# Byte offsets of TensorE's operands in SBUF: equal steps for the weight slots, h shifted by 16 bytes from FFN to FFN, each buffer of g by 32 bytes

## The chip, the cores and the metric

The kernel runs on one core of one Trainium2 chip. The metric is the device time of the whole program in microseconds, the median of several runs. One execution was also recorded by the hardware profiler.

## The reference, cut to what matters

The program is a decoder trunk of two layers on 512 tokens of 1024 channels. Each layer is an FFN, a token mixer and another FFN; the first mixer is a causal pooling, the second an attention with a forget gate. A norm with shift and scale stands before each of the six sublayers, numbered 0 to 5, so that the FFNs are 0, 2, 3 and 5, the pooling is 1 and the attention is 4:

```
h = rms_norm(x) * gain * (1 + scale) + shift
x = x + 0.5 * (1 + gate) * ((silu(h @ w_g) * (h @ w_u)) @ w_out)        # FFN, width 2816
```

All of it is in float32.

## The kernel before

**Precision.** A matmul takes float32r operands, of fewer bits than float32. Every operand is therefore split into a high part (rounded) and a low part (the rest), and `mm3` (lines 162 to 165) makes three matmuls of each product: high weight with high data (L163), high weight with low data (L164), low weight with high data (L165). The standing operand, 128 x 128, is loaded ahead of each matmul; the streaming operand has 512 or 256 columns.

**Layout.** Channels lie on the 128 partitions, tokens along the free dimension. h, the normed input, is a pair of tiles `hhi` and `hlo` of 8 blocks of 512 tokens; `norm` (lines 210 to 220) writes them in two halves of 256 tokens. g, the gated hidden values, is a pair of tiles of 512 tokens for each of the 22 blocks of the FFN's width, in nine rotating buffers each for the high and the low part.

**An FFN** (`ffn`, from line 258, and `closing`) goes through the width in three chunks of 8, 8 and 6 blocks. In `up` each block is 48 matmuls: gate and up projection, 8 blocks of channels, three products; the text calls these 48 a column block. The first two or three blocks of FFNs 2, 3 and 5 are done in two halves of 256 tokens, all others in 512 columns. After a chunk, the down product streams g: for each of 8 output blocks 24 matmuls. The last chunk's down product, `closing`, has 18 matmuls for each output block, in two halves of 256 columns (FFN 5: one of 512).

**Weights** come from DRAM to a `raw` tile, and ScalarE and VectorE split them into a slot, a pair of tiles `wh` and `wl` of 8 KB a partition each (`slot`, lines 67 to 71). FFNs 0, 2 and 3 rotate over three slots, two in the pool `wts` and one in the pool `more`; FFN 5 and the attention rotate over the two of `wts`. The first four blocks of FFN 0 use these three and a fourth pair, `w4`. In the attention the projections to q, k and v have h standing and the weights streaming, 256 columns wide; the forget gate has its weights `fh` and `fl` standing and h streaming.

**Where tiles lie.** Pools are stacked in the order in which they are opened, from the left (low addresses) or the right (high addresses), each tile on a multiple of 32 bytes. From the right: `top` with h, then `right` with `cond` (4096 bytes), then `more`. From the left: `pers`, `tmp`, `wts`, then the pools of each stage, g's among them. The start addresses that follow, in bytes of a partition, with the remainder modulo 512:

| tiles | address | modulo 512 |
|---|---|---|
| hhi, hlo | 196576, 212960 | 480 |
| wh, wl of the two slots in `wts` | 43808, 52000, 60192, 68384 | 288 |
| wh, wl of the slot in `more` | 176096, 184288 | 480 |
| g, first buffer (FFNs 0 and 2; 3 and 5) | 92960; 125728 | 288 |
| first weights of the attention, `w` | 92960 and on | 288 |
| fh, fl | 145248, 149344 | 352 |
| w4 | 154432, 162624 | 320 |

Block strides inside these tiles (512 bytes for the FFNs' weights, 1024 for those of the projections, 2048 for h and g's buffers) keep the remainder.

**Order.** SyncE's queue, which issues all DMAs, is in the order of the program's text in the FFNs; the other engines' order is a scheduler's, by a modelled timeline, except for the beginning, where ScalarE and VectorE are in the order of the text too.

Of the kernel before, what the change touches and what calls it, by code (L numbers as in the profile page):

```python
# [7 lines left out]
F32 = mybir.dt.float32  # L8
F32R = mybir.dt.float32r
# [6 lines left out]
P = 128  # L16
D = 1024
KT = D // P
S = 512
# [3 lines left out]
JC = 8  # L23
# [10 lines left out]
LAG = 3  # L34
SPAN = 16
EARLY = 4
WHOLE = ((0, S),)
HALVES = ((0, S // 2), (S // 2, S // 2))

# [2 lines left out]
def trunk(  # L42
# [6 lines left out]
    pe, act, dve, gp = nc.tensor, nc.scalar, nc.vector, nc.gpsimd  # L49

    top = ctx.enter_context(tc.tile_pool(name="top", bufs=1, side="right"))
    hhi = top.tile([P, KT, S], F32R, name="hhi")
    hlo = top.tile([P, KT, S], F32R, name="hlo")
    adas = ExitStack()
    right = adas.enter_context(tc.tile_pool(name="right", bufs=1, side="right"))
    pers = ctx.enter_context(tc.tile_pool(name="pers", bufs=1))
    tmp = ctx.enter_context(tc.tile_pool(name="tmp", bufs=2))
    wts = ctx.enter_context(tc.tile_pool(name="wts", bufs=2))
    ps = ctx.enter_context(tc.tile_pool(name="ps", bufs=5, space=PSUM))
    pss = ctx.enter_context(tc.tile_pool(name="pss", bufs=3, space=PSUM))  # L60
# [3 lines left out]
    def bank(tag="mm"):  # L64
        return banks[tag].tile([P, S], F32, tag=tag, name=tag)
# [89 lines left out]
    def weights(src, shape, pieces=4):  # L155
        raw = wts.tile(shape, F32, tag="raw", name="raw")
        nc.sync.dma_start(raw, src)
        parts = slot(shape)
        split(parts, raw, pieces)
        return parts  # L160

    def mm3(o, lh, ll, rh, rl, start, stop):
        pe.matmul(o, lh, rh, start=start, stop=False)  # L163
        pe.matmul(o, lh, rl, start=False, stop=False)  # L164
        pe.matmul(o, ll, rh, start=False, stop=stop)  # L165
# [42 lines left out]
        return r  # L208

    def norm(i, acc, t0, tn, summed=False):  # L210
        sl = slice(t0, t0 + tn)
        r = rsig(acc, t0, tn, summed)
        for kt in range(KT):
            a, s = (mods[i][c][:, kt:kt + 1] for c in "as")
            t1 = tmp.tile([P, tn], F32, tag="t1", name="t1")
            dve.scalar_tensor_tensor(out=t1, in0=x[:, kt, sl], scalar=a, in1=r[:, :tn],
                                     op0=ALU.mult, op1=ALU.mult)
            act.activation(hhi[:, kt, sl], t1, AF.Identity, bias=s)
            dve.scalar_tensor_tensor(out=hlo[:, kt, sl], in0=t1, scalar=s,
                                     in1=hhi[:, kt, sl].bitcast(F32), op0=ALU.add, op1=ALU.subtract)  # L220
# [11 lines left out]
    def new_acc():  # L232
        return tmp.tile([P, S], F32, tag="acc", name="acc", bufs=1)
# [24 lines left out]
    def ffn(i, feed, jobs, then, begin=None, ahead_by=2, started=None):  # L258
        jobs = list(jobs)
        loaded = []  # L260

        def job(pool, behind):

            if loaded:
                work, raw = loaded.pop()
                with tc.issue_after(behind):
                    work(raw)
                if ahead_by == 1:
                    return
            if jobs:  # L270
                load, work = jobs.pop(0)
                loaded.append((work, load(pool)))

        acc = new_acc() if then else None
        with (
            tc.tile_pool(name=f"ffn{i}", bufs=2, reuse_waits="tile") as fp,
            tc.manual_schedule(engines={mybir.EngineType.SP}),
            ExitStack() as early,
        ):
            ap = early.enter_context(tc.tile_pool(name=f"ada{i}", bufs=ahead_by, reuse_waits="tile"))  # L280

            def g_tile():
                return (fp.tile([P, S], F32R, tag="gh", name="gh", bufs=JC + 1),
                        fp.tile([P, S], F32R, tag="gl", name="gl", bufs=JC + 1))

            def gated(gu, g, t0, tn):
                sl = slice(t0, t0 + tn)
                sil = fp.tile([P, S], F32, tag="sil", name="sil")
                act.activation(sil[:, :tn], gu[0][:, :tn], AF.Silu)  # L289
                dve.tensor_tensor(out=sil[:, :tn], in0=sil[:, :tn], in1=gu[1][:, :tn], op=ALU.mult)  # L290
                act.activation(g[0][:, sl], sil[:, :tn], AF.Copy)  # L291
                return dve.tensor_tensor(out=g[1][:, sl], in0=sil[:, :tn], in1=g[0][:, sl].bitcast(F32),
                                         op=ALU.subtract)

            def up(wt, g, t0, tn):
                wh, wl = wt
                sl = slice(t0, t0 + tn)
                gu = []
                for k in range(2):
                    o = bank()  # L300
                    for kt in range(KT):
                        mm3(o[:, :tn], wh[:, k, kt], wl[:, k, kt], hhi[:, kt, sl], hlo[:, kt, sl],
                            kt == 0, kt == KT - 1)
                    gu.append(o)
                return gated(gu, g, t0, tn)

            for ci, (j0, nj) in enumerate(CHUNKS):
                g = []
                ready = 0
                if ci == 0:  # L310
                    ready = started or feed.depth
                    g = [g_tile() for _ in range(ready)]
                    if begin is not None:
                        begin(g, gated)
                        feed.fetch(feed.depth)
                        nc.sync.dma_start(x, x_in)
                        job(ap, None)
                    else:
                        head, feed.made = feed.made, []
                        for t0, tn in HALVES:  # L320
                            for j in range(ready):
                                up(head[j], g[j], t0, tn)
                                if t0:
                                    feed.fetch()
                for j in range(j0 + ready, j0 + nj):
                    wt = feed.take()
                    g.append(g_tile())
                    done = up(wt, g[-1], 0, S)
                    if j >= 3:
                        job(ap, done.ins)  # L330
                if ci < 2:
                    for dt in range(KT):
                        wh, wl = feed.take()
                        y = bank()
                        for f in range(nj):
                            mm3(y, wh[:, f], wl[:, f], g[f][0], g[f][1], f == 0, f == nj - 1)
                        done = dve.scalar_tensor_tensor(  # L337
                            out=x[:, dt, :], in0=y, scalar=mods[i]["g"][:, dt:dt + 1],
                            in1=x[:, dt, :], op0=ALU.mult, op1=ALU.add)
                        job(ap, done.ins)  # L340
                else:
                    while jobs or loaded:
                        job(ap, done.ins)
                    early.close()
                    feed.fetch(len(feed.units))
                    closing(feed.made, 6, g, i, acc, then)

    def closing(wt, n, g, i, acc, then):

        for t0, tn in HALVES if then else WHOLE:  # L350
            sl = slice(t0, t0 + tn)
            for dt in range(KT):
                y = bank()
                for f in range(n):
                    (wh, wl), at = wt[(dt * n + f) // 16], (dt * n + f) % 16
                    mm3(y[:, :tn], wh[:, at], wl[:, at], g[f][0][:, sl], g[f][1][:, sl], f == 0,
                        f == n - 1)
                update(y[:, :tn], i, dt, t0, tn, acc)
            if then:
                then(acc, t0, tn)  # L360
# [88 lines left out]
    def fox(i, early_pool, first, second_half, then):  # L449
        acc2 = new_acc()  # L450
        with tc.tile_pool(name="fox", bufs=1, reuse_waits="tile") as fp:
# [205 lines left out]
            def early(ots):  # L657
# [3 lines left out]
                def step(dt):  # L661
                    y = bank("s")
                    for k in range(EARLY):
                        u, at = divmod(dt * EARLY + k, 16)
                        if at == 0:
                            held["w"] = weights(fox_o[u], [P, 16, P])
                        wh, wl = held["w"]
                        mm3(y, wh[:, at], wl[:, at], ots[k][0], ots[k][1], k == 0, k == EARLY - 1)
                    dve.scalar_tensor_tensor(
# [13 lines left out]
            for grp in range(NG):  # L683
                nxt, steps = projections(grp + 1) if grp + 1 < NG else (None, [])
                if grp == NG - 1:
                    steps = early(ots)
                    ots = ots[EARLY:]
                ots += attend(made, grp, steps)
                made = nxt
            closing([weights(fox_o[u], [P, 16, P]) for u in range(EARLY // 2, KT // 2)], KT - EARLY,  # L690
                    ots, i, acc2, then)
# [3 lines left out]
    with tc.tile_pool(name="more", bufs=1, side="right", reuse_waits="tile") as more:  # L695
# [78 lines left out]
        def begin(g, gated):  # L774
            for j in range(4):
                gated(gu[j], g[j], 0, S)
# [118 lines left out]
```

## Time and profile before

| | us |
|---|---|
| median of three runs (lowest, highest) | 1857.13 (1853.2, 1859.62) |
| profiled execution | 1856.85 |
| its span, first to last instruction | 1855.1 |
| TensorE busy with matmuls | 1822.1 (98%) |
| weight loads, beside the matmuls | 1543.5 (83%) |
| VectorE, ScalarE, GpSimd busy | 985.9, 622.5, 106.9 |

The mean granted clock of TensorE is 0.99 of full speed. The chain of work that ended last is 96% TensorE, 85% of it in the three lines of `mm3` with banks of the tag `mm`. [...]

### The profile page before, as it was taken

How to read it: one execution, taken by the hardware profiler on the slowest of the kernel's cores; microseconds unless marked ns; L12 is line 12 of the kernel's file. 1: busy time of each engine (PE TensorE's matmuls, PEld its weight loads, DVE VectorE, ACT ScalarE, POOL GpSimd, SP SyncE). 2: the span in 40 equal slices, each digit the busy share in tenths (PEclk: the TensorE clock that was granted, in tenths of full speed). 3: DMA queues.
4: the chain of work that ended last, by engine and by line, in shares of the span. 5: the costliest groups of instructions: out<-in, count | busy, mean ns of one | idle time of the engine just before them, and what ended most of it. 6: DMA issues, size and time to landing. Idle time of an engine off the chain costs nothing.

```text
span 1855.1 us, 23985 instructions
## 1 busy us (share of the span) xinstructions
PE 1822.1 (98%) x9564; PEld 1543.5 (83%) x9564; DVE 985.9 (53%) x1947; ACT 622.5 (34%) x1242; POOL 106.9 (6%) x118
## 2 busy tenths in 40 slices
PE   6999999989999999999999999999999999999999
PEld 5888888879888888998888889988997888888887
DVE  7467466386466473363554534666676653432433
ACT  6323223244213232242222333354444442222221
POOL 0000000040000000110000001321010200000000
PEclk9999999989999999999999999999999899999999
DMA  9457466211366452131543431022211121321321
GB/s 365 183 202 265 174 234 225 92 69 66 117 252 243 171 216 94 69 137 69 204 164 131 183 126 69 33 70 80 69 64 63 38 100 57 127 102 56 136 92 68
DMA packets 45712, 244.66 MB, mean 132 GB/s; under 512 B 5392, under 2 KB 9872, under 8 KB 21792
## 3 DMA queue, kind: packets, MB, share of 16 engines
q1 hardware_dynamic: 45600, 243.13, 35.8%
q8 instruction: 75, 1.23, 0.3%
q14 instruction: 37, 0.30, 0.0%
HBM read 240.98 MB, written 2.13 MB: 131 GB/s over the span
## 4 chain that ended last, share of the span: by engine, by line
PE 96%; DVE 2%; ACT 0%; DMA 0%; issue 0%; SPq 0%; POOL 0%; ACTq 0%; POOLq 0%
PE mm L163 29%; PE mm L164 28%; PE mm L165 28%; PE s L163 3%; PE s L164 3%; PE s L165 3%; PE mm L600 1%; PE mm L583 1%; PE mm L422 1%; DVE wl L152 1%; DMA rows<-x_rows 0%; DVE x L225 0%; PE s L543 0%; PE mm L181 0%; DVE win L396 0%; PE s L207 0%
## 5 line engine op out<-in xcount | busy, mean ns | idle before, releaser
L164 PE MATMUL mm<-hlo,wh 128*128 128x512 f32 (+1 forms) x1512 | 566.0, 376 | 2.5 <-DVE hlo L764 2.5
L165 PE MATMUL mm<-hhi,wl 128*128 128x512 f32 (+1 forms) x1512 | 564.5, 376 | 0.5 <-DVE wl L152 0.5
L163 PE MATMUL mm<-hhi,wh 128*128 128x512 f32 (+1 forms) x1512 | 560.1, 375 | 1.8 <-ACT hhi L755 1.4
L151 ACT ACTIVATE wh<-raw 128x256 fp32r<-128x256 f32 (+2 forms) x528 | 311.3, 654 | 572.4 <-PE mm L164 324.5
L152 DVE TENSOR_TENSOR wl<-raw,wh 128x256 fp32r<-128x256 f32 (+2 forms) x528 | 359.8, 733 | 50.5 <-ACT wh L151 46.4
L164 PEld LDWEIGHTS mm<-hlo,wh 128*128 128x128 f32 x1512 | 284.3, 188 | 58.7 <-DVE hlo L764 3.0
L165 PEld LDWEIGHTS mm<-hhi,wl 128*128 128x128 f32 x1512 | 284.5, 188 | 56.5 <-DVE wl L152 0.7
L163 PEld LDWEIGHTS mm<-hhi,wh 128*128 128x128 f32 x1512 | 282.5, 188 | 58.2 <-ACT hhi L755 1.8
L290 DVE TENSOR_TENSOR sil<-sil,mm 128x512 f32<-128x512 f32 (+1 forms) x95 | 61.0, 642 | 481.1 <-PE mm L165 473.3
L164 PE MATMUL mm<-gl,wh 128*128 128x512 f32 (+1 forms) x848 | 299.1, 353 | 0.0
L165 PE MATMUL mm<-gh,wl 128*128 128x512 f32 (+1 forms) x848 | 298.0, 353 | 0.0
L163 PE MATMUL mm<-gh,wh 128*128 128x512 f32 (+1 forms) x848 | 297.8, 354 | 0.0
L165 PEld LDWEIGHTS mm<-gh,wl 128*128 128x128 f32 x848 | 159.9, 189 | 22.4
L164 PEld LDWEIGHTS mm<-gl,wh 128*128 128x128 f32 x848 | 160.0, 189 | 22.2
L163 PEld LDWEIGHTS mm<-gh,wh 128*128 128x128 f32 x848 | 159.3, 189 | 22.7
L100 DVE CUSTOM_DVE_ANT_0 ada<-ada,cond 128x1024 f32<-128x1024 f32 x144 | 170.1, 1218 | 0.7 <-DMA ada<-ada_w 0.7
L289 ACT ACTIVATE sil<-mm 128x512 f32<-128x512 f32 (+1 forms) x94 | 52.7, 561 | 254.6 <-PE mm L165 253.3
L337 DVE SCALAR_TENSOR_TENSOR x<-mm,mg,x 128x512 f32<-128x512 f32 x64 | 47.9, 749 | 105.3 <-PE mm L165 104.8
L175 POOL TENSOR_TENSOR acc<-acc,sq 128x256 f32<-128x256 f32 x56 | 49.5, 884 | 870.9 <-ACT sq L174 535.3
L163 PE MATMUL s<-wh,hhi 128*128 128x256 f32 x288 | 84.0, 292 | 1.9 <-DVE qk L549 1.9
L291 ACT ACTIVATE gh<-sil 128x512 fp32r<-128x512 f32 (+1 forms) x96 | 56.1, 585 | 76.6 <-DVE sil L290 76.6
L165 PE MATMUL s<-wh,hlo 128*128 128x256 f32 x288 | 81.6, 283 | 0.0
(177 smaller groups left out, 1728.3 us busy)
## 6 DMA issues: line engine op xcount, KB each, us to landing
raw<-w_in SPq DMA_DIRECT2D x84, 1024.0 KB, 5.0
ada<-ada_w SPq DMA_DIRECT2D x72, 1024.0 KB, 4.9
raw<-w_out SPq DMA_DIRECT2D x64, 512.0 KB, 5.6
raw<-w_end SPq DMA_DIRECT2D x12, 1024.0 KB, 4.8
raw<-fox_qkv SPq DMA_DIRECT2D x12, 1024.0 KB, 4.8
raw<-w_in SPq DMA_DIRECT2D x16, 256.0 KB, 8.3
cb<-cum SPq DMA_DIRECT2D x16, 256.0 KB, 3.3
raw<-fox_o SPq DMA_DIRECT2D x4, 1024.0 KB, 4.9
```

The costliest lines, as they stand in the source:

```text
L100: dve.tensor_tensor_reduce(out=raw[:, r, :], in0=raw[:, r, :], in1=cond, scale=1.0, scalar=0.0, op0=ALU.mult, op1=ALU.add, accum_out=mods[ ...
L151: act.activation(hi[:, c:c + n], src[:, c:c + n], AF.Copy)
L152: dve.tensor_tensor(out=lo[:, c:c + n], in0=src[:, c:c + n], in1=hi[:, c:c + n].bitcast(F32), op=ALU.subtract)
L163: pe.matmul(o, lh, rh, start=start, stop=False)
L164: pe.matmul(o, lh, rl, start=False, stop=False)
L165: pe.matmul(o, ll, rh, start=False, stop=stop)
L175: gp.tensor_tensor(out=acc[:, sl], in0=acc[:, sl], in1=sq, op=ALU.add)
L289: act.activation(sil[:, :tn], gu[0][:, :tn], AF.Silu)
L290: dve.tensor_tensor(out=sil[:, :tn], in0=sil[:, :tn], in1=gu[1][:, :tn], op=ALU.mult)
L291: act.activation(g[0][:, sl], sil[:, :tn], AF.Copy)
L337: done = dve.scalar_tensor_tensor(out=x[:, dt, :], in0=y, scalar=mods[i]["g"][:, dt:dt + 1], in1=x[:, dt, :], op0=ALU.mult, op1=ALU.add)
L422: pe.matmul(y[:, :tn], self.w[:, 2 * dt + ct], made[dt // 2][:, ct], start=ct == 0, stop=ct == 1)
```

## The change

Three things are done, all to where tiles lie. An unused tile of 48 floats, `gap`, stands between `tmp` and `wts`. h becomes one tile, `h_room`, longer by 16 floats, from which `h_tiles` cuts the pair at a start that depends on the sublayer: float 16 (FFN 0 and the attention), 12 (FFN 2), 8 (FFN 3), 4 (FFN 5). The buffers of g are longer by 8 floats, and the 512 that are used begin at float 0, 2, 4 or 6 in FFNs 0, 2, 3 and 5.

```
--- before.py
+++ after.py
@@ -34,6 +34,10 @@
 LAG = 3
 SPAN = 16
 EARLY = 4
+H_ROOM = 16
+H_AT = {2: 12, 3: 8, 5: 4}
+G_ROOM = 8
+G_AT = {0: 0, 2: 2, 3: 4, 5: 6}
 WHOLE = ((0, S),)
 HALVES = ((0, S // 2), (S // 2, S // 2))
 
@@ -49,12 +53,21 @@
     pe, act, dve, gp = nc.tensor, nc.scalar, nc.vector, nc.gpsimd
 
     top = ctx.enter_context(tc.tile_pool(name="top", bufs=1, side="right"))
-    hhi = top.tile([P, KT, S], F32R, name="hhi")
-    hlo = top.tile([P, KT, S], F32R, name="hlo")
+    h_room = top.tile([P, 2 * KT * S + H_ROOM], F32R, name="h")
+
+    def h_tiles(i):
+
+        at = H_AT.get(i, H_ROOM)
+        both = h_room[:, at:at + 2 * KT * S].rearrange("p (c k t) -> p c k t", c=2, t=S)
+        return both[:, 0], both[:, 1]
+
+    hhi, hlo = h_tiles(0)
     adas = ExitStack()
     right = adas.enter_context(tc.tile_pool(name="right", bufs=1, side="right"))
     pers = ctx.enter_context(tc.tile_pool(name="pers", bufs=1))
     tmp = ctx.enter_context(tc.tile_pool(name="tmp", bufs=2))
+    gap = ctx.enter_context(tc.tile_pool(name="gap", bufs=1))
+    gap.tile([P, 48], F32, name="gap")
     wts = ctx.enter_context(tc.tile_pool(name="wts", bufs=2))
     ps = ctx.enter_context(tc.tile_pool(name="ps", bufs=5, space=PSUM))
     pss = ctx.enter_context(tc.tile_pool(name="pss", bufs=3, space=PSUM))
@@ -208,6 +221,9 @@
         return r
 
     def norm(i, acc, t0, tn, summed=False):
+        nonlocal hhi, hlo
+        if t0 == 0:
+            hhi, hlo = h_tiles(i)
         sl = slice(t0, t0 + tn)
         r = rsig(acc, t0, tn, summed)
         for kt in range(KT):
@@ -280,8 +296,8 @@
             ap = early.enter_context(tc.tile_pool(name=f"ada{i}", bufs=ahead_by, reuse_waits="tile"))
 
             def g_tile():
-                return (fp.tile([P, S], F32R, tag="gh", name="gh", bufs=JC + 1),
-                        fp.tile([P, S], F32R, tag="gl", name="gl", bufs=JC + 1))
+                return [fp.tile([P, S + G_ROOM], F32R, tag=t, name=t, bufs=JC + 1)[:, G_AT[i]:G_AT[i] + S]
+                        for t in ("gh", "gl")]
 
             def gated(gu, g, t0, tn):
                 sl = slice(t0, t0 + tn)
```

## Rows read from the trace of the kernel before

**Rows 1.** The page: the span, and TensorE's share of it.

```profile
span 1855.1 us, 23985 instructions
...
PE 1822.1 (98%) x9564; PEld 1543.5 (83%) x9564; DVE 985.9 (53%) x1947; ACT 622.5 (34%) x1242; POOL 106.9 (6%) x118
```

**Rows 2.** TensorE's waits: us, times, longest; the longest, and that for h.

```profile
PE s L738 <- DVE rows L745: 12.1, 1, 12.1
...
PE mm L163 <- ACT hhi L218: 0.2, 1, 0.2
```

**Rows 3.** Windows: busy (count), clock, DMA share, GB/s; around pooling, FFN 2, 5.

```profile
357.00:462.00 105.00, 97.56 (x686) 0.93 0.18 62
462.00:758.00 296.00, 296.00 (x1288) 1.00 0.48 181
1508.00:1852.00 344.00, 343.41 (x1487) 1.00 0.27 94
```

**Rows 4.** Groups of TensorE by form: busy us, mean ns; h and g.

```profile
L163 PE MATMUL mm<-hhi,wh 128*128 128x512 f32 x1256 | 491.7, 394 | 1.4 <-ACT hhi L755 1.4
...
L163 PE MATMUL mm<-gh,wh 128*128 128x512 f32 x560 | 217.8, 390 | 0.0
```

**Rows 5.** Timeline (start, duration), FFN 2: column blocks, 48 matmuls apart.

```profile
472.99 0.40 PE L163 MATMUL mm<-hhi,wh 128*128 128x512 f32 x1
...
484.19 0.40 PE L163 MATMUL mm<-hhi,wh 128*128 128x512 f32 x1
...
495.38 0.39 PE L163 MATMUL mm<-hhi,wh 128*128 128x512 f32 x1
...
506.29 0.40 PE L163 MATMUL mm<-hhi,wh 128*128 128x512 f32 x1
```

**Rows 6.** Timeline, FFN 5, h on both slots, 192 matmuls apart.

```profile
1518.71 0.39 PE L163 MATMUL mm<-hhi,wh 128*128 128x512 f32 x1
...
1563.51 0.39 PE L163 MATMUL mm<-hhi,wh 128*128 128x512 f32 x1
```

**Rows 7.** Timeline, FFN 2, g on `wts`, then on `more`, 24 apart.

```profile
533.93 0.39 PE L163 MATMUL mm<-gh,wh 128*128 128x512 f32 x1
...
539.37 0.39 PE L163 MATMUL mm<-gh,wh 128*128 128x512 f32 x1
...
544.87 0.39 PE L163 MATMUL mm<-gh,wh 128*128 128x512 f32 x1
```

**Rows 8.** Timeline, FFN 2, h, 256: 24 on `wts`, 18 `more`, 24 `wts`.

```profile
439.57 0.28 PE L163 MATMUL mm<-hhi,wh 128*128 128x256 f32 x1
...
442.29 0.28 PE L163 MATMUL mm<-hhi,wh 128*128 128x256 f32 x1
...
445.01 0.28 PE L163 MATMUL mm<-hhi,wh 128*128 128x256 f32 x1
...
447.17 0.28 PE L163 MATMUL mm<-hhi,wh 128*128 128x256 f32 x1
...
450.77 0.28 PE L163 MATMUL mm<-hhi,wh 128*128 128x256 f32 x1
...
453.60 0.28 PE L163 MATMUL mm<-hhi,wh 128*128 128x256 f32 x1
```

**Rows 9.** Timeline, FFN 2, g on `wts`, 256 columns, 18 apart.

```profile
773.30 0.28 PE L163 MATMUL mm<-gh,wh 128*128 128x256 f32 x1
...
775.46 0.28 PE L163 MATMUL mm<-gh,wh 128*128 128x256 f32 x1
```

**Rows 10.** Timeline, projections: first of 24, and what follows the last.

```profile
1172.25 0.28 PE L163 MATMUL mm<-w,hhi 128*128 128x256 f32 x1
...
1175.08 0.38 PE L207 MATMUL s<-dg,ones 128*128 128x256 f32 x1
```

**Rows 11.** Timeline, forget gate: first of 22, and what follows the last.

```profile
1191.09 0.40 PE L165 MATMUL mm<-hhi,fl 128*128 128x512 f32 x1
...
1196.22 0.28 PE L163 MATMUL mm<-w,hhi 128*128 128x256 f32 x1
```

More of the change, by code (lines that the diff above doesn't have):

```diff
@@ L36 @@
 EARLY = 4
+H_ROOM = 16
+H_AT = {2: 12, 3: 8, 5: 4}
+G_ROOM = 8
+G_AT = {0: 0, 2: 2, 3: 4, 5: 6}
 WHOLE = ((0, S),)
@@ L51, in trunk, with h_tiles @@
     top = ctx.enter_context(tc.tile_pool(name="top", bufs=1, side="right"))
-    hhi = top.tile([P, KT, S], F32R, name="hhi")
-    hlo = top.tile([P, KT, S], F32R, name="hlo")
+    h_room = top.tile([P, 2 * KT * S + H_ROOM], F32R, name="h")
+    def h_tiles(i):
+        at = H_AT.get(i, H_ROOM)
+        both = h_room[:, at:at + 2 * KT * S].rearrange("p (c k t) -> p c k t", c=2, t=S)
+        return both[:, 0], both[:, 1]
+    hhi, hlo = h_tiles(0)
     adas = ExitStack()
@@ L57, in trunk @@
     tmp = ctx.enter_context(tc.tile_pool(name="tmp", bufs=2))
+    gap = ctx.enter_context(tc.tile_pool(name="gap", bufs=1))
+    gap.tile([P, 48], F32, name="gap")
     wts = ctx.enter_context(tc.tile_pool(name="wts", bufs=2))
@@ L210, in norm @@
     def norm(i, acc, t0, tn, summed=False):
+        nonlocal hhi, hlo
+        if t0 == 0:
+            hhi, hlo = h_tiles(i)
         sl = slice(t0, t0 + tn)
@@ L282, in g_tile @@
             def g_tile():
-                return (fp.tile([P, S], F32R, tag="gh", name="gh", bufs=JC + 1),
-                        fp.tile([P, S], F32R, tag="gl", name="gl", bufs=JC + 1))
+                return [fp.tile([P, S + G_ROOM], F32R, tag=t, name=t, bufs=JC + 1)[:, G_AT[i]:G_AT[i] + S]
+                        for t in ("gh", "gl")]
             def gated(gu, g, t0, tn):
```

## The prediction

> **What bounds the kernel now.** I read the page's head first: TensorE is busy in 1822.1 of 1855.1 us [rows 1]. The profiled execution took 1856.85 us, so 1.8 us lie around its span; it stands 0.28 us under the median of the three timed runs, 1857.13 us, so sums made against the one hold for the other. Next the waits of TensorE by releaser: the longest, 12.1 us, is at the start, and the wait for `norm` is 0.2 us [rows 2]. [...] The only thing left to change is the pace at which matmuls follow each other, and the change touches nothing but byte addresses.
>
> A matmul's own duration hides the pace: 394 ns for h and 390 ns for g, of the same 128x512 shape [rows 4], and consecutive ones overlap. The pace is read from start to start. In FFN 2 one column block of 48 matmuls lasts 11.20 us, the next 11.19, the third 10.91 [rows 5]: 233.3, 233.1 and 227.3 ns for each. The third is the one whose weights lie in the slot of pool `more`; the slots rotate in threes. In FFN 5, which has only the two slots of `wts`, 192 matmuls take 44.80 us, 233.3 ns each, throughout [rows 6]. Transposed roles are seen in the down product: with g streaming, 24 matmuls take 5.44 us on a `wts` slot (226.7 ns) and 5.50 us on the `more` slot (229.2 ns) [rows 7].
>
> **Offsets.** All tiles concerned are built of rows whose strides are multiples of 512 bytes, so one remainder modulo 512 describes a tile. From the layout before: h 480, `wts` slots 288, `more` 480, g 288. Taking weight minus moving operand modulo 256: h on `more` 0 (227.3 ns), g on `wts` 0 (226.7), h on `wts` 64 (233.3), g on `more` 192 (229.2). The 22 matmuls of the forget gate whose weights lie 128 away take 5.13 us, 233.2 ns [rows 11]. Equal offsets are the quickest seen at 512 columns. At 256 columns they are the slowest: 120.0 ns for h on `more` and for g on `wts`, against 113.3 and 117.9 ns for h on `wts` [rows 8, 9]; one pair of addresses shows two paces, so the pace also depends on what ran before.
>
> **What the change does to them.** The unused `gap` tile moves everything on the left by 192 bytes: `wts` goes from 288 to 480. The new h tile is 64 bytes longer, and the pools below it on the right move down by as much: `more` goes from 480 to 416. So the slots do not all end at one offset modulo 512 or 128, only modulo 64, as before. h is at 480 in FFN 0 and the attention layer, 464 in FFN 2, 448 in FFN 3, 432 in FFN 5. Buffer b of g is at 480 + 32b (high part) and 256 + 32b (low part), plus 0, 8, 16, 24 by FFN. No instruction is added, removed or reordered in the source; no queue sees a different DMA list.
>
> **Term by term.** Counts are from the code; the rows have 1256 h and 560 g matmuls of 512 columns for each of the three products [rows 4], and the code has 24 more of h in banks of another name.
>
> h at 512 columns on `wts`: 672 in FFN 0, 624 in FFN 2, 576 in FFN 3, 960 in FFN 5. FFN 0 becomes the equal pair: 672 x (227.3 - 233.3) = -4.0 us (bounds -4.0 and 0). FFNs 2, 3 and 5 get weights 16, 32 and 48 bytes beyond h, which no row shows; they lie between 0 (227.3) and 64 (233.3), so I take half: 2160 x -3.0 = -6.5 us (bounds -13.0 and 0).
>
> h on `more`, 960 matmuls: from 0 to -64, -48 and -32. Nearest is g on `more`, 229.2 (it is at -64): 960 x 1.9 = +1.8 us (bounds 0 and, at 233.3, +5.8).
>
> g at 512 columns: 1296 on `wts` at 226.7 and 384 on `more` at 229.2. The new offsets walk evenly round the 256 bytes, so I take the mean of the four distances seen, (226.7 + 229.2 + 233.3 + 233.2) / 4 = 230.6: 1296 x 3.9 + 384 x 1.4 = +5.6 us (bounds -1.0, all at 226.7, and +10.1, all at 233.3).
>
> Attention's q, k and v projections, 1152 matmuls of 256 columns with h standing and weights streaming: 117.9 ns before (24 in 2.83 us) [rows 10], equal afterwards, so 120.0: 1152 x 2.1 = +2.4 us (bounds: +2.4, and at 113.3 -5.3).
>
> 256 columns in the FFNs: g on `wts` (576) and h on `more` (192) leave the equal pair, 120.0 to 117.9, -1.6 us; h on `wts` in FFN 2 (192) comes close to it, +0.4 us. Together -1.2 us (bounds -5.1, all 768 at 113.3, and +3.9, all 576 of h on `wts` from 113.3 to 120.0).
>
> The two halves of h become one tile, and `norm` writes the next FFN's h over a shifted copy of the last. I cost it at nothing: the wait for `norm` is 0.2 us [rows 2], and the readers of the old h are over by a whole down product. If tracking became coarser, the place is the stretch around the pooling layer, where TensorE already idles 105.00 - 97.56 = 7.4 us [rows 3]; I hold up to 7 us more for it. [...]
>
> Sum: -4.0 - 6.5 + 1.8 + 5.6 + 2.4 - 1.2 = -1.9 us, so 1855.2 us, rounded to 1855.
>
> [...]
>
> **The rivals.** (A) Near is as good as equal: 16 to 48 bytes still count as one line. For: equal and 64 away are the only steps seen below. Against: nothing shows a flat part. The second term is then -13.0 and the third +0.6 (FFN 0 alone): -4.0 - 13.0 + 0.6 + 5.6 + 2.4 - 1.2 = -9.6, 1847.5 us.
> (B) The pace belongs to the pair of memory regions, not to the offset: h and `more` both lie high, g and `wts` both low, and the slow pairs are mixed, so rows 5 to 7 fit this as well. The change then does nothing: 1857 us.
> (C) Only exact equality pays, the other side. FFNs 2, 3 and 5 keep 233.3, h on `more` leaves its equal pair for 233.3, g spreads: -4.0 + 0 + 5.8 + 5.6 + 2.4 - 1.2 = +8.6, 1865.7 us. It decides as soon as a weight 16 bytes off paces like one 64 off. For: the forget gate, 128 away, is no better than 64. Against: g on `more` is only 2.5 ns off equal.
> (D) It doesn't do what it says: the `more` slots do move, as above; that is already in the third term, and with them at 480 that term would be smaller, 0 in FFN 0: -0.6 us.
>
> **How the numbers follow.** Chances: the sum 0.42, A 0.27, B 0.14, C 0.14, and 0.03 for a new wait. A measurement of this kernel tells about 0.3%, 5.6 us, from no change. Faster by more: 0.24 of A and 0.12 of the sum's own spread, 0.36. Slower by more: C's 0.13 and 0.04 of the rest, 0.17. Within: 0.47. The likeliest case has its own range, 1850 to 1861. For 8 in 10 I reach into A and C: 1845 to 1866. The bounds of all terms together (-28 to +22) are wider, but they would need every unknown on one side.
>
> **What would show it.** Start to start in the four FFNs, slot by slot: FFN 0 on `wts` at 227 (else B); FFNs 2, 3, 5 at about 228.8, 230.3 and 231.8 (all 227: A; all 233: C); h on `more` at 228 to 230; g no longer at one pace but different from buffer to buffer, about 230.6 in the mean; the projections at 120. Idle time of TensorE unchanged near 33 us; more of it would be the new wait. The forecast is wrong if any new offset goes below 226.7 ns or above 233.3, for the rows give no pace outside these.

## The result, and the profile after

The changed kernel takes 1868.74 us (median of five, 1862.84 to 1869.45) against 1857.13 (1853.2 to 1859.62): 1.0054 of the time before, 95% interval 1.0034 to 1.0074. It is slower by some 11 us, above the range forecast (1845 to 1866). The profiled execution after took 1863.08 us, only 6.2 us more than the one before. Executions of either kernel differ by some 6 us, those with the higher mean granted clock being the shorter (after: 1863 us at 0.995, 1869 at 0.992; before, in the runs beside e9: 1853 at 0.995, 1859 at 0.991), and the profile after is one of the shorter. In the matmuls that the change touches the two profiles differ by 11.8 us, about what the medians say.

The page of the kernel after, the lines that answer to [rows 1]:

```profile
span 1861.3 us, 23984 instructions
...
PE 1827.1 (98%) x9564; PEld 1544.7 (83%) x9564; DVE 987.4 (53%) x1947; ACT 622.4 (33%) x1242; POOL 107.0 (6%) x118
```

TensorE's waits after (line waited for: us, times, longest), as [rows 2]:

```profile
PE s L754 <- DVE rows L761: 12.4, 1, 12.4
...
PE mm L176 <- ACT h L234: 0.2, 1, 0.2
```

TensorE has the same 9564 matmuls and is idle for 1861.3 - 1827.1 = 34.2 us, before 33.0. The wait for `norm` is 0.2 us as before: making h one tile cost nothing. The windows after (length, TensorE busy and count, the other engines, clock, DMA share, GB/s), FFN 2 and FFN 5 as in [rows 3]:

```profile
466.00:760.00 294.00, 294.00 (x1275) 239.55 (x1274) 156.82 (x264) 79.59 (x143) 0.00 (x0) 1.00 0.47 172
1520.00:1858.00 338.00, 337.64 (x1443) 271.37 (x1441) 114.46 (x176) 85.98 (x151) 0.00 (x0) 1.00 0.26 90
```

TensorE is still busy throughout there, in 294.00 of 294.00 and 337.64 of 338.00 us, at a granted clock of 1.00, as before. So the loss is pace. The groups by form after (busy us, mean ns of one), as [rows 4]:

```profile
L176 PE MATMUL mm<-h,wh 128*128 128x512 f32 x1256 | 492.2, 394 | 1.6 <-ACT h L771 1.6
...
L176 PE MATMUL mm<-gh,wh 128*128 128x512 f32 x560 | 220.5, 395 | 0.0
```

A g matmul now lasts 395 ns instead of 390, an h matmul 394 as before: the table points at g and hides what h does, since quicker and slower layers cancel in the mean. The starts show it. The timeline after (start us, us, engine, line, what), first of each block of 24 unless said, in FFN 0 (`more` at 79.90, `wts` at 90.89, 72 apart), FFN 2 (as [rows 5]), FFN 3, and FFN 5 (144 apart, as [rows 6]):

```profile
79.90 0.39 PE L176 MATMUL mm<-h,wh 128*128 128x512 f32 x1
...
85.40 0.39 PE L176 MATMUL mm<-h,wh 128*128 128x512 f32 x1
...
90.89 0.39 PE L176 MATMUL mm<-h,wh 128*128 128x512 f32 x1
...
107.21 0.39 PE L176 MATMUL mm<-h,wh 128*128 128x512 f32 x1
...
480.48 0.40 PE L176 MATMUL mm<-h,wh 128*128 128x512 f32 x1
...
486.16 0.40 PE L176 MATMUL mm<-h,wh 128*128 128x512 f32 x1
...
491.83 0.40 PE L176 MATMUL mm<-h,wh 128*128 128x512 f32 x1
...
497.44 0.40 PE L176 MATMUL mm<-h,wh 128*128 128x512 f32 x1
...
503.03 0.39 PE L176 MATMUL mm<-h,wh 128*128 128x512 f32 x1
...
508.47 0.39 PE L176 MATMUL mm<-h,wh 128*128 128x512 f32 x1
...
951.58 0.40 PE L176 MATMUL mm<-h,wh 128*128 128x512 f32 x1
...
957.18 0.40 PE L176 MATMUL mm<-h,wh 128*128 128x512 f32 x1
...
1531.59 0.40 PE L176 MATMUL mm<-h,wh 128*128 128x512 f32 x1
...
1565.38 0.40 PE L176 MATMUL mm<-h,wh 128*128 128x512 f32 x1
```

Per matmul: FFN 0 on `wts`, the equal pair, (107.21 - 90.89) / 72 = 226.7 ns, on `more` 5.50 / 24 = 229.2. FFN 2 on `wts`, 16 bytes off, shows two paces at one distance: 5.68 / 24 = 236.7 before this block on `more` (5.61 / 24 = 233.8) and 5.44 / 24 = 226.7 after it. (An earlier block on `more`, at 458 us, had left it at 236.7.) FFN 3, 32 bytes off: 233.3. FFN 5, 48 off: 33.79 / 144 = 234.7, worse than the 233.3 of 64 off before.

The same view of g (FFN 0 and FFN 2, 24 apart, [rows 7]) and of the first projections (24 apart, [rows 10]):

```profile
134.84 0.40 PE L176 MATMUL mm<-gh,wh 128*128 128x512 f32 x1
...
140.38 0.39 PE L176 MATMUL mm<-gh,wh 128*128 128x512 f32 x1
...
525.13 0.40 PE L176 MATMUL mm<-gh,wh 128*128 128x512 f32 x1
...
530.74 0.40 PE L176 MATMUL mm<-gh,wh 128*128 128x512 f32 x1
...
1174.11 0.28 PE L176 MATMUL mm<-w,h 128*128 128x256 f32 x1
...
1176.99 0.38 PE L220 MATMUL s<-dg,ones 128*128 128x256 f32 x1
```

g: 5.54 / 24 = 230.8 ns in FFN 0, 5.61 / 24 = 233.8 in FFN 2; it was 226.7 on `wts`. The projections: 2.88 / 24 = 120.0 ns, 117.9 before.

The ledger below is worked out from the starts of all matmuls of both traces, each start-to-start time put to its layer, operand, width and slot; it holds the terms of the prediction against what they came to. FFN 0's first blocks are included; they run interleaved, and which slot a step there is put to moves FFN 0's two terms by some half a microsecond.

```
term (us)                          forecast   came to
h 512 on wts, FFN 0                  -4.0      -4.4
h 512 on wts, FFNs 2, 3, 5           -6.5      -0.6   (-1.8, -0.1, +1.3)
h 512 on more                        +1.8      +4.5   (FFN 0 +0.8, 2 +1.6, 3 +2.1)
g 512                                +5.6      +7.9   (FFN 0 +1.3, 2 +2.1, 3 +1.1, 5 +3.4)
projections                          +2.4      +3.1
256 columns in the FFNs              -1.2      +1.3
sum                                  -1.9     +11.8
```

The rest of the profiled difference, 6.2 - 11.8 = -5.6 us, lies in attention's other matmuls (-4.0) and in those of the pooling layer and its norms (-1.6), where the execution after was granted more clock: 0.99 against 0.98 from 1120 to 1500 us, 0.98 against 0.93 from 357 to 460.

### The profile page after: what moved, and what is told of

It reads as the page before. It is cut to its first block, busy times and chain, and to the rows that moved or that the text cites. A ratio compares the mean times of both kernels' runs of the same rounds, so it can differ in the third digit from the quotient of the medians.

```text
span 1861.3 us, 23984 instructions
## 1 busy us (share of the span) xinstructions
PE 1827.1 (98%) x9564; PEld 1544.7 (83%) x9564; DVE 987.4 (53%) x1947; ACT 622.4 (33%) x1242; POOL 107.0 (6%) x118
## 4 chain that ended last, share of the span: by engine, by line
PE 96%; DVE 2%; ACT 1%; DMA 0%; issue 0%; POOL 0%; SPq 0%; ACTq 0%; DVEq 0%; POOLq 0%
PE mm L176 29%; PE mm L177 28%; PE mm L178 28%; PE s L176 3%; PE s L177 3%; PE s L178 3%; PE mm L616 1%; PE mm L599 1%; DVE wl L165 0%; DMA rows<-x_rows 0%; DVE x L241 0%; PE mm L438 0%; PE s L559 0%; DVE win L412 0%; DVE ada L113 0%; DVE t L403 0%
## 5 line engine op out<-in xcount | busy, mean ns | idle before, releaser
L177 PE MATMUL mm<-h,wh 128*128 128x512 f32 (+1 forms) x1512 | 566.8, 376 | 1.7 <-DVE h L780 1.7
L178 PE MATMUL mm<-h,wl 128*128 128x512 f32 (+1 forms) x1512 | 564.4, 375 | 0.5 <-DVE wl L165 0.5
L176 PE MATMUL mm<-h,wh 128*128 128x512 f32 (+1 forms) x1512 | 560.8, 376 | 2.0 <-ACT h L771 1.6
L177 PEld LDWEIGHTS mm<-h,wh 128*128 128x128 f32 x1512 | 284.7, 189 | 57.1 <-DVE h L780 2.3
L178 PEld LDWEIGHTS mm<-h,wl 128*128 128x128 f32 x1512 | 284.8, 189 | 55.7 <-DVE wl L165 0.7
L176 PEld LDWEIGHTS mm<-h,wh 128*128 128x128 f32 x1512 | 282.8, 188 | 58.1 <-ACT h L771 1.8
L176 PE MATMUL s<-wh,h 128*128 128x256 f32 x288 | 85.1, 295 | 1.9 <-DVE qk L565 1.9
L178 PE MATMUL s<-wh,h 128*128 128x256 f32 x288 | 82.6, 287 | 0.0
L177 PE MATMUL s<-wl,h 128*128 128x256 f32 x288 | 82.4, 286 | 0.0
```

## The experiments

Theory from here on: each block's pace is set by one number, the bytes from the streamed operand to the weights modulo 256; only equality is quick at 512 columns, and no distance near it is a cheaper form of it. Each kernel is the change with the edits shown. All times are beside the kernel before, run on the same chip in turn with them.

**Everything equal, at two absolute places.**

```
e1:  H_ROOM = 0;  H_AT = {};  G_ROOM = 0;  G_AT all 0        h, g, all slots at 480 mod 512
e2:  as e1, but H_ROOM = 120, default at = 0, gap 56 floats   h, g, all slots at 0
```

> The change with nothing but its gap: h is not lengthened or shifted and g's buffers are not lengthened, so h, g and all three slots lie at 480 modulo 512 in every FFN. Theory 'exact equality pays': every 512-column matmul of h and g at 226.7 ns; 2832 of h on the wts slots gain 6.6 ns each (-18.7 us), 384 of g on the more slot 2.4 (-0.9), projections lose 3.1 us, the 864 matmuls of 256 columns that become equal lose 3.8 us; in sum about -13 us, 1844 us against 1857. Rival 'the quick pace of FFN 0 belonged to the pair of tiles or to that stretch': FFN 5, all on wts slots, stays at 233 and the time at 1855 to 1860 us.

> As e1_equal, with everything moved so that h, g and all slots lie at 0 modulo 512 and not at 480. Theory 'only the distance counts': the same paces as e1_equal, 226.7 and 120.0 ns, and the same time within 3 us, about 1844 us. Rival 'lines of 64 bytes count': a stream that starts on a line needs one line of 16 columns less, 220.0 ns for 512 columns and 113.3 for 256, about 5600 x 6.7 + 3000 x 6.7 ns = 57 us less than e1_equal.

Measured: 1840.68 us, 0.9915 of before (0.9902 to 0.9928), and 1839.93 us, 0.9913 (0.9898 to 0.9927). Both are some 3 to 4 us under what was expected, and the rival of e2, 57 us less than e1, falls. So the gap alone, without the change's shifts, makes the kernel 16 us faster than before, and the shifts turn that into 12 us slower. The timeline of e1, FFN 5, h on `wts`, 168 matmuls apart:

```profile
1519.69 0.39 PE L176 MATMUL mm<-h,wh 128*128 128x512 f32 x1
...
1557.77 0.39 PE L176 MATMUL mm<-h,wh 128*128 128x512 f32 x1
```

38.08 / 168 = 226.7 ns, where [rows 6] had 233.3. The same of e2, 144 apart:

```profile
1521.77 0.39 PE L176 MATMUL mm<-h,wh 128*128 128x512 f32 x1
...
1554.41 0.39 PE L176 MATMUL mm<-h,wh 128*128 128x512 f32 x1
```

32.64 / 144 = 226.7 as well: at equal offsets the two places tried pace alike. Both kernels have the projections at 119.6 ns in the mean and the 256-column blocks of the FFNs at 120: equality is dear there, as [rows 8, 9] said with 120.0 against 113.3 and 117.9.

**More distances of h.** Gap, equal g, all weight slots at one offset; h at another distance in each FFN.

```
e3:  H_ROOM = 128;  H_AT = {0: 64, 2: 96, 3: 126, 5: 124}     256, 128, 8, 16 bytes
e4:  H_ROOM = 128;  H_AT = {0: 4, 2: 127, 3: 125, 5: 80}      -16, 4, 12, 192
e11: H_ROOM = 128;  H_AT = {0: 104, 2: 122, 3: 88, 5: 100}    96, 24, 160, 112
```

> All slots and g at 480 modulo 512; h so placed that the weights lie 256 bytes beyond it in FFN 0, 128 in FFN 2, 8 in FFN 3, 16 in FFN 5. Theory 'the distance counts modulo 256': 226.7, 233.3, and for 8 and 16 between 227 and 237, with 16 in one of two paces, 226.7 or 236.5, as in FFN 2 of the changed kernel. Rival 'modulo 512': 256 is no better than 233. Rival 'modulo 128': 128 and 256 both 226.7.

> All slots and g at 480 modulo 512; weights 16 bytes before h in FFN 0, 4 bytes beyond in FFN 2, 12 in FFN 3, 192 in FFN 5. Theory 'words of 16 bytes must meet': 4 and 12 lie in the same or the next word and pace at 226.7 to 230, -16 at 230 to 237, 192 at 229 as g on the more slot did. Rival 'any distance but 0 breaks the step': 4 and 12 at 233 or more.

> Gap and equal g, weights of all slots at one offset, and h at distances not seen so far: weights minus h 96 bytes in FFN 0, 24 in FFN 2, 160 in FFN 3, 112 in FFN 5 (modulo 256). Theory (only equal offsets, and 16 in one of its two phases, give 226.7; everything else is 229 to 240): h at 512 columns between 228.9 and 237 in all four, time 1855 to 1863. Rival (the pace is a curve that rises evenly with the distance and falls back towards 256): 24 at about 228, 96 to 160 the slowest, at 233 or more.

Measured, one execution each: 1858.28, 1866.53 and 1868.02 us. In e3 both rivals fall: 256 bytes off is quick (226.7 ns) and 128 (233.3) is not. In e4 the theory of 16-byte words falls with 12 bytes off (240.0 ns, below); the rival, everything but 0 at 233 or more, falls with 4 bytes (230.6). In e11 the evenly rising curve falls, 24 bytes being as slow as 112 and 160 (233.3 ns each). e11's time lies above its forecast; its paces do not, so it was the sum that I made too small. Its timeline, FFN 0 (96 off) and FFN 2 (24 off), 24 apart:

```profile
97.54 0.39 PE L176 MATMUL mm<-h,wh 128*128 128x512 f32 x1
...
103.16 0.40 PE L176 MATMUL mm<-h,wh 128*128 128x512 f32 x1
...
497.42 0.40 PE L176 MATMUL mm<-h,wh 128*128 128x512 f32 x1
...
503.02 0.40 PE L176 MATMUL mm<-h,wh 128*128 128x512 f32 x1
```

5.62 / 24 = 234.2 and 5.60 / 24 = 233.3 ns. The dearest pair is in e4, FFN 3, 12 bytes off:

```profile
949.02 0.41 PE L176 MATMUL mm<-h,wh 128*128 128x512 f32 x1
...
954.78 0.41 PE L176 MATMUL mm<-h,wh 128*128 128x512 f32 x1
```

5.76 / 24 = 240.0. And in e3, FFN 0, a whole 256 bytes off, 48 apart, is as quick as equal, 10.88 / 48 = 226.7:

```profile
90.75 0.39 PE L176 MATMUL mm<-h,wh 128*128 128x512 f32 x1
...
101.63 0.39 PE L176 MATMUL mm<-h,wh 128*128 128x512 f32 x1
```

The steady paces of h at 512 columns in the FFNs, all runs of this document, ns, worked out from the starts:

```
weights - h (mod 256)   0      4      8      12         16                   24
                        226.7  230.6  232.0  239-240    226.7, 233.3, 236.7  233.3
                        32     48     64     96     112    128    160    192
                        233.3  234.7  233.3  234.2  233.3  233.3  233.3  228.9
                        -48           -32    -16
                        230.1, 233.3  233.4  231.7
```

This is no ramp from 0 to 64. Twelve bytes off is worse than sixty-four, and the eight distances measured from 24 to 160 all lie at 233 to 235. Distances met at two places agree: 128 in the forget gate of before and in e3 (233.2 and 233.3 ns), 192 in the change's FFN 0 and in e4 (228.9). At 4, 8, 12 and 24 bytes the weights stood at 480 only, so there the distance and h's own place moved together, and no run parts them.

**The change's two parts apart.**

```
e5:  H_ROOM = 0;  H_AT = {}                       gap and spread of g alone
e9:  G_ROOM = 0;  G_AT all 0                      gap and shift of h alone
```

> The change's gap and its spread of g, without any shift of h (h, all weight slots at one offset; g walks by 32 bytes per buffer plus 0, 8, 16, 24 by FFN). Theory (the pace is set by the distance of weights and streamed operand modulo 256, each block by itself): h keeps 226.7 ns at 512 columns, g comes to about 231 ns in FFNs 0 and 3 and 233 to 234 in FFNs 2 and 5; 1680 matmuls of g at 4 to 7 ns more than 226.7 make about +8 us over the run with the gap alone, so 1848 to 1849 us. Rival (the spread of g is harmless and only the shift of h costs): 1841. Rival (the two parts only cost together): 1841 as well, with g at 226.7.

> The change without its spread of g: gap, h at 0, 16, 32, 48 bytes from wts in the four FFNs, more 64 bytes lower, all buffers of g at one offset equal to wts. Theory (the two parts add, each matmul group paces by its own distance): against the run with the gap alone, h costs +18 us by the blocks of the change's own trace (FFN 0 +2, FFN 2 +4, FFN 3 +5, FFN 5 +7.5) and g on more +1 us, so 1858 to 1861 us, h at 226.7 / 226.7 and 236.7 / 233.3 / 234.7 in FFNs 0, 2, 3, 5 and g on wts at 226.7. Rival (the slow h in the change is an after-effect of the spread g that runs between): h below 230 in FFNs 2 and 5 and a time near 1848.

Measured: e5 1850.45 us, 0.9971 (0.9959 to 0.9984); e9 1860.06 us, 1.0018 (1.0009 to 1.0028). Both theories of a sole culprit fall: on top of the gap alone (-0.85% against before) g's spread costs 0.56% and h's shift 1.03%. Together they would make +0.74%; the change has +0.54%, 3.7 us less, no more than the four intervals together leave open. Of that 1.8 us are seen in FFN 2, where h on `wts` has 233.3 ns in the mean in e9 (every block after the first down product is there) and 230.4 in the change, and 0.9 us is g on `more` (384 x 2.3 ns), which e9 slows as well and which is so counted twice. e5 is 1.5 us above its forecast, e9 within it but for FFN 2, whose second pace was to be 226.7. The timeline of e5, FFN 2, h 96 apart and g 24 apart:

```profile
485.40 0.39 PE L176 MATMUL mm<-h,wh 128*128 128x512 f32 x1
...
507.16 0.39 PE L176 MATMUL mm<-h,wh 128*128 128x512 f32 x1
...
523.79 0.40 PE L176 MATMUL mm<-gh,wh 128*128 128x512 f32 x1
...
529.42 0.40 PE L176 MATMUL mm<-gh,wh 128*128 128x512 f32 x1
```

21.76 / 96 = 226.7 for h and 5.63 / 24 = 234.6 for g: the spread of g costs in the down products and does not touch an h at equal offsets. An h 16 bytes off it does touch, as FFN 2 of e9 and of the change show: there h on `wts` has 230.4 ns in the mean with the spread of g and 233.3 without.

**The unequal slots of `more` as the excuse.**

```
e6:  H_ROOM = 64;  H_AT = {2: 60, 3: 56, 5: 52}   more at the distance of wts in every FFN
```

> The change, with h's tile made so much longer that the slots of pool more really stand at the same distance modulo 256 to h as those of wts do (0, 16, 32, 48 bytes in FFNs 0, 2, 3, 5); g as in the change. Theory (distance modulo 256 alone, 16, 32 and 48 pay nothing): h on more goes to 226.7 in FFN 0 (144 matmuls, -0.3 us) and to the pace of wts in the others; 1866 to 1868 us. Rival (the change is slow since its slots are not equal after all): about 1855, the time forecast for the change.

Measured: 1876.06 us, 1.0105 (1.0086 to 1.0124), slower than the change, where the forecast had slightly faster and the rival 1855. FFN 0's `more` went to 226.7 as expected (288 matmuls outside the first blocks, -0.6 us; the forecast counted 144). The miss is FFN 2, h, first of 48, `wts` at 482.26, `more` at 493.62, `wts` again at 504.98:

```profile
482.26 0.40 PE L176 MATMUL mm<-h,wh 128*128 128x512 f32 x1
...
493.62 0.40 PE L176 MATMUL mm<-h,wh 128*128 128x512 f32 x1
...
504.98 0.40 PE L176 MATMUL mm<-h,wh 128*128 128x512 f32 x1
```

236.7 ns throughout (11.36 / 48 twice). With all blocks of h 16 bytes off, h never came into its quick pace; the change had 226.7 in 8 of its 13 blocks on `wts`, each time from a block on `more`, which stood elsewhere, to the next down product. By the starts FFN 2 is 5.0 us slower than in the change, of 7.3 us between the medians (9.5 by the two ratios); the profiled execution also had a lower clock in attention (0.97 in 1120 to 1500 us, 0.99 in the change), and how the rest divides is not settled.

**Is the pace a state that stays?**

```
e10:  H_AT = {2: 12, 3: 12, 5: 12};  G_ROOM = 0;  G_AT all 0   16 off in FFNs 2, 3 and 5
```

> As the run without the spread of g, but h 16 bytes from wts in FFN 3 and FFN 5 too (FFN 3 with slots of more 48 bytes below h, FFN 5 with none). Theory of a kept phase: two runs of blocks at one distance of 16 differ since a row of matmuls stays in the phase that it starts in, 236.7 ns, until blocks of another distance push it into the other, 226.7; so FFN 3 shows 236.7 first and 226.7 after blocks on more, as FFN 2, and FFN 5, where nothing comes between, 236.7 throughout. Rival (the pace is a fixed function of the layer's addresses): FFN 3 and FFN 5 at one and the same pace. Time 1856 to 1863.

Measured: 1858.49 us, one execution, within the forecast. Its timeline, h on `wts`, 24 apart: FFN 3 after a block on `more` (848.43) and after down products of g (941.73); FFN 5 before its first down product (1525.30) and after it (1631.14):

```profile
848.43 0.39 PE L176 MATMUL mm<-h,wh 128*128 128x512 f32 x1
...
853.87 0.39 PE L176 MATMUL mm<-h,wh 128*128 128x512 f32 x1
...
941.73 0.40 PE L176 MATMUL mm<-h,wh 128*128 128x512 f32 x1
...
947.33 0.40 PE L176 MATMUL mm<-h,wh 128*128 128x512 f32 x1
...
1525.30 0.40 PE L176 MATMUL mm<-h,wh 128*128 128x512 f32 x1
...
1530.98 0.40 PE L176 MATMUL mm<-h,wh 128*128 128x512 f32 x1
...
1631.14 0.40 PE L176 MATMUL mm<-h,wh 128*128 128x512 f32 x1
...
1636.74 0.40 PE L176 MATMUL mm<-h,wh 128*128 128x512 f32 x1
```

226.7, 233.3, 236.7 and 233.3 ns from one distance. The fixed function is out: the same layer and the same addresses pace differently by what ran before. I had FFN 5 at 236.7 throughout, and forgot that g's down products come between its blocks; they moved it to 233.3, where it then stayed to the end of the layer. (e3's FFN 5, also 16 off, had already made the same step, 236.7 to 233.3, at its first down product.) FFN 3 went from 236.7 to 226.7 over a block on `more`, as expected, and after its first down product to 233.3, which was not. That the pace stays until a block of another distance comes holds in every block of this run; which pace follows which block was not worked out.

**Towards a better version.** The projections and two closing down products at a distance that is better for 256 columns.

```
e7:  e2 with H_AT = {4: 48}                              attention's h 192 bytes off
e8:  e7 with the last chunk's g of FFNs 0 and 2 64 bytes on
```

> As the run with everything at 0 modulo 512, but attention's h 192 bytes on, so that the 1152 matmuls of the projections (256 columns, h standing) are 192 bytes apart from their weights. Theory (at 256 columns the equal pair is not the best: 119.6 ns for the projections at equal offsets, 117 at 192): 1152 x 2.6 ns = -3.0 us against that run, 1837. Forget gate and other 512-column uses of h in attention may lose up to 24 x 6.6 ns = 0.2 us. Rival (projections don't depend on the offset of the standing operand in this way): 1840, with the projections at 119.6.

> As the run before it, and the last chunk's g in FFNs 0 and 2, whose 256-column down products run at 120.0 ns on equal offsets, 64 bytes on, so that weights and g are 192 apart. Theory: 576 matmuls of 256 columns from 120.0 to between 113.3 and 117.7, -1.3 to -3.8 us, and nothing at 512 columns, 1833 to 1836 us; if the last chunk has down products of 512 columns too, they go from 226.7 to 228.9. Rival (the pace at 256 columns is the same at all offsets of g): 1837, as the run before it.

Measured: 1838.5 us, 0.9912 (0.9897 to 0.9927), and 1837.67 us, 0.9903 (0.9886 to 0.9920). The blocks did what was asked: projections from 119.6 to 117.0 ns (worth 2.1 us by the starts, 3.0 forecast), the closing products from 120 to 117.8 (1.2 us). The medians follow the forecast's sign and lie 1.5 us above the one forecast and 1.7 above the range of the other, but the intervals of e1, e2, e7 and e8 overlap, so the last two steps are shown in the trace and not in the time. By the ratios all four beat the kernel before by 0.85 to 1.0% and the change by 1.4 to 1.5%.

## Why the prediction was wrong, by its own steps

- **Bound, and addresses as the lever: right.** TensorE is busy in all of FFN 2 (294.00 of 294.00 us), no wait came (idle 34.2 us for 33.0), and the addresses alone moved the time. The distance modulo 256 is the variable (with, at 16 and at -48, what ran before): e3's FFN 0, 256 bytes off, is as quick as equal (226.7 ns), and by e1 and e2 the absolute place made no difference between the two tried (226.7 ns in both). One shape, 128x512, runs at 226.7 (e1) to 240.0 ns (e4) with only offsets moved. Why the distance counts, no run shows.
- **The step that failed: "they lie between 0 (227.3) and 64 (233.3), so I take half".** It drew a line between two points and put the change's new distances on it. The forecast was 228.8, 230.3 and 231.8 ns for 16, 32 and 48 bytes by the list of what would show it; the trace has 236.7 or 226.7, 233.3 and 234.7, and with paces above 233.3 the forecast's own sign of being wrong came up. The curve is not monotone, so neither end was a bound: FFN 5 alone came to +1.3, above the 0 that was taken as the worst case, though the sum of the term, -0.6, stayed inside "-13.0 and 0". Cost: 5.9 of the 13.7 us by which the sum was off.
- **h on `more`, mis-sized.** The nearest row was at 64 below, 229.2, and I gave it to 48 and 32 below too. FFN 0, truly 64 below, came to 229.0 in the mean; FFN 2 to 230.0 to 233.3 by block and FFN 3 to 233.4. +4.5 for +1.8.
- **g, mis-sized.** The mean of four distances, 230.6, fits FFNs 0 and 3 (230.7 to 231.1 in the mean of a layer and slot), where every buffer stands a multiple of 16 bytes off. In FFNs 2 and 5 the 8 and 24 bytes by FFN leave remainders of 8, and those take 233.1 to 233.9. No row of before had a distance that was not a multiple of 64. +7.9 for +5.6.
- **256 columns in the FFNs: wrong in sign**, +1.3 for -1.2. g on `more` was at 113.3 to 116.2 ns in the mean of a layer, stalls left out, and went to 117.9 to 119.8; h in FFN 5 went from 113.9 to 119.0. I had costed what leaves the equal pair and not what leaves a better one.
- **FFN 0 and the projections: right**, -4.4 for -4.0 and +3.1 for +2.4 (the one column read, 117.9 ns, stood above the projections' mean of 116.8).
- **The rivals.** (C), only exact equality pays, 1865.7 us, comes nearest, in its mechanism and its time (h on `more` was not quite at its 233.3, g above it in two FFNs); I gave it 0.14 because g on `more` was near equal. That was 192, at 228.9 the cheapest unequal distance of the table that shows a single pace, and said nothing of the others. (A) would have needed 227 at 16, 32 and 48; (B), memory regions, falls with FFN 0, where h high and `wts` low run at 226.7; (D) was right in FFN 0, where e6 took `more` from 229.0 to 226.7 for the 0.6 us priced, but as an excuse it falls: with `more` at the distance of `wts` everywhere the kernel was slower.
- **The range** reached 1866 because I held all-terms-high to be unlikely. Three of the four terms that missed read one unknown curve at 512 columns, low at 0 and at 229 to 240 at nearly every other distance, and so they missed together; the fourth, 256 columns, missed the same way for a reason of its own.

## What to carry to other kernels

Where TensorE is saturated, take the pace from start to start per pair of tiles, and for matmuls of 512 columns lay streamed operand and weights at the same offset modulo 256; here that alone was worth 0.9% (e1, e2: 226.7 ns where before had 233.3), the 256-column matmuls losing by it (119.6 to 120 where before, 64 bytes off, had 113.3 to 117.9). Do not interpolate a cost over addresses: measure the distance itself, and take "near" to be as far as any other until a row shows it. When a term has two known points, what lies between them is a rival of its own, and terms that read one unknown curve miss together.

## What the runs showed that was not expected

- At 16 bytes off h has three steady paces, 226.7, 233.3 and 236.7 ns (all three in e10), and there keeps the one that it has over whole column blocks until matmuls of another distance come between. Equal offsets settled at 226.7 ns: h in the change's FFN 0, in e1, e2, e5 and, 256 off, e3; g on `wts` in before.
- Small distances are not the cheap ones: 230.6 ns at 4 bytes (e4), 232.0 at 8 (e3), 239 to 240 at 12 (e4), beside 226.7 at 0. In the change g is quicker where its buffers stand multiples of 16 bytes off (231 ns, FFNs 0 and 3) than with remainders of 8 (233 to 234, FFNs 2 and 5); h has no such order: 4 bytes off is quicker than 32 to 160 (233.3 to 234.7).
- At 256 columns the order turns: equal is the slow end (120.0 ns, [rows 8, 9]; 8 bytes off (e3), 24 and 160 (e11) are no better, and only 12 (e4) is slower, 121.6 to 122.2), 4 bytes off (e4) is at 116.7, and 64 (before) and 192 (before, e7, e8) at 113.3 to 118.
